# Recurrence of a two-layer hybrid backbone: both heads' keys in the same columns, products as 128x64 tiles, substitution in blocks of 4

## The chip, the cores and the metric

The kernel runs on one core of a Trainium2 chip. The metric is the device time of one execution in microseconds (us). The engines that matter are TensorE (PE; its weight loads are listed as PEld), VectorE (DVE), ScalarE (ACT), GpSimd (POOL) and SyncE (SP), which issues the transfers.

## The reference, cut to what matters

Two layers run over 512 latent tokens and, in the first layer, 256 context tokens as well. Each layer has a mixer (an RWKV-7 recurrence in both directions, windowed attention and a Fourier mix, merged by gates) and a gated ConvFFN. The change concerns the recurrence alone:

```python
def wkv_scan(state0, feat, d, reverse):
    r, v, kk, decays, keys, removals, _ = feat
    def step(S, inp):
        r_t, w_t, k_t, v_t, kk_t, b_t = inp
        sa = jnp.einsum("bhvk,bhk->bhv", S, -kk_t)
        S = S * w_t[:, :, None, :] + sa[..., :, None] * b_t[..., None, :] + v_t[..., :, None] * k_t[..., None, :]
        return S, jnp.einsum("bhvk,bhk->bhv", S, r_t)
```

There are four heads of 64 channels, forward and backward. The kernel works in chunks of 64 tokens: inside a chunk the recurrence is the solution of a unit lower triangular 64x64 system, so that each chunk, head and direction needs the products of its keys with its queries, a triangular inverse, and a few small matmuls that carry the state from chunk to chunk.

## The kernel before, in words

The tokens go through the recurrence in six windows of two chunks in each layer (`mix`, L1329): twelve windows in all. For each window three functions run.

`wkv_features` (L779) runs once per window and loops over the two directions `d`: 24 direction passes. Heads lie in pairs on the partitions: head `h` of a pair has rows 64h to 64h+63, and `k` counts the two pairs. A pass makes decays on ACT and DVE (L822 to L838) and then multiplies them in. `W1[h]` (L851 on DVE, L853 on POOL) holds a head's queries in its own 64 rows; its other rows are zeroed first (L809). `BK` holds both heads' keys; the two kinds of key (`na` and `kf`) lie in crossed column halves for the two heads, so that L854 and L855 are written for each head by itself, as 64-partition instructions. Then L864 makes the products: for each head a bank `ps` takes four matmuls (`q`: two chunks by two pairs) of a 128x128 weight tile of `BK`, with `m` columns moving (128, or 64 where no output is wanted: the first two windows of layer 1, four passes). Out of each bank L869 writes one half of `MR` and L870 one half of the other head's rows of `W1`, both under the triangular mask `gmask` (DVE). POOL then scales `BK` in place (L872).

`wkv_inverse` (L897) runs once per window and inverts all triangles of the window at once. L909 lays out 16x16 diagonal blocks, one per partition. The loop L914 to L919 is a substitution over the 16 rows: for each of 15 columns one multiply (L917) and one add (L919) over what lies below it, 30 dependent DVE instructions. Two transposes (L929, L930) bring the result back, and small 32-row matmuls on PE (L938 to L977) join the 16-blocks to 32 and then to 64.

`wkv_prep` (L980) runs once per chunk, 24 times. It transposes the values (L987) and the scaled keys (L997, four PE transposes of 128x128 into one bank), which ACT copies to `BT`. `wkv_step` (L1002) then carries the state (L1021 to L1063); its matmuls already are 128x64 or 64x64 tiles, put side by side in the array by `tile_position`. While the recurrence runs there are two banks for the tag `x` (the banks `ps`, `pp`, `pv`, `pb` and those of the inverse), one for `y` and five for the projections (L1599).

The order of the work is not written out by hand. Recurrence pieces stand under `tc.high_priority()` (L1369, L1452); the projections and gate matmuls of the same layer (L177 to L179, weights split into a high and a low part by L106 and L118) follow in the program text, and a planner puts them between the recurrence's instructions, by its own estimates, before the run. Each engine then executes its list strictly in that order, and waits on semaphores where an operand is not there yet.

Of the kernel before, what the change touches and what calls it, by code (L numbers as in the profile page):

```python
# [11 lines left out]
ALU = mybir.AluOpType  # L12
AX = mybir.AxisListType
# [50 lines left out]
class Kern:  # L64
# [714 lines left out]
    def wkv_features(self, l, w, F, P, wp, wt):  # L779

        nc = self.nc
        x = P["x"]
        NC = 2
        WT = NC * CH
        W = {}
# [8 lines left out]
        def rows(t, h):  # L794
            return t[64 * h:64 * h + 64]

        for d in range(2):
# [5 lines left out]
            def tok(t):  # L803
                return flip(t[:, :, lo:lo + WT])
# [41 lines left out]
            split = lambda a: a.rearrange("p k (c t) -> p k c t", t=CH)  # L846
            for h in range(2):
                ww = rows(W1[h], h).rearrange("p c k t -> p k c t")
                bk = rows(BK, h).rearrange("p c k t -> p k c t")
                o = 64 * h  # L850
                nc.vector.tensor_tensor(ww[:, :, :, 0:64], split(rows(tok(F["kk"]), h)), rows(e1, h)[:, :, :, 0:64], ALU.mult)  # L851
                if need_y:
                    nc.gpsimd.tensor_tensor(ww[:, :, :, 64:128], split(rows(tok(F["r"]), h)), rows(e1, h)[:, :, :, 1:65], ALU.mult)  # L853
                nc.vector.tensor_tensor(bk[:, :, :, o:o + 64], split(rows(na, h)), split(rows(e2, h)), ALU.mult)  # L854
                nc.vector.tensor_tensor(bk[:, :, :, 64 - o:128 - o], split(rows(kf, h)), split(rows(e2, h)), ALU.mult)  # L855
            vs = self.t(wp, [128, 2, WT + CH], "vs_", bufs=4)
            nc.gpsimd.memset(vs[0:64, :, 0:64], 0.0)
            nc.gpsimd.memset(vs[64:128, :, WT:WT + 64], 0.0)
            self.act(vs[0:64, :, 64:64 + WT], tok(F["v"])[0:64])
            self.act(vs[64:128, :, 0:WT], tok(F["v"])[64:128])  # L860
            for h in range(2):
                ps = self.ps()
                for q in range(4):
                    nc.tensor.matmul(ps[:, q * 128:q * 128 + m], lhsT=BK[:, q // 2, q % 2, :],  # L864
                                     rhs=W1[h][:, q // 2, q % 2, 0:m], start=True, stop=True)
                pv = ps.rearrange("p (q t) -> p q t", q=4)[:, :, 0:m]
                oth = 1 - h
                mask = lambda z: rows(self.gmask, z)[:, 0:m].unsqueeze(1).broadcast_to((64, 4, m))
                nc.vector.tensor_tensor(rows(MR, h)[:, 4 * d:4 * d + 4, 0:m], rows(pv, h), mask(h), ALU.mult)  # L869
                nc.vector.tensor_tensor(rows(W1[h], oth).rearrange("p c k t -> p (c k) t")[:, :, 0:m], rows(pv, oth),  # L870
                                        mask(oth), ALU.mult)
            nc.gpsimd.tensor_tensor(  # L872
                BK, BK, e1[:, :, :, 64].rearrange("p k c -> p c k").unsqueeze(3).broadcast_to((128, NC, 2, 128)), ALU.mult)
            W[d] = (W1, BK, vs, e1)
# [22 lines left out]
    def wkv_inverse(self, MR, wp):  # L897
# [3 lines left out]
        mm = nc.tensor.matmul  # L901
        NI = 8
        Fm = self.t(wp, [128, 16, 32], "iv", bufs=3)
        F16 = self.t(wp, [128, 16, 16], "F16", bufs=1)
        T = self.t(wp, [128, 16, 16], "T16", bufs=1)
        tmp = self.t(wp, [128, 64], "itmp", bufs=1)
        m0, m1, r1 = (self.lmask[:, z:z + 1] for z in (0, 1, 2))

        nc.vector.transpose(Fm.rearrange("l t s -> l (t s)"), MR[:, :, 0:64].rearrange("q i (b t) -> q t b i", b=4))  # L909
        nc.gpsimd.memset(T, 0.0)  # L910
        nc.gpsimd.memset(T.rearrange("l t j -> l (t j)")[:, ::17], 1.0)
        nc.vector.tensor_scalar(F16, Fm[:, :, 0:16], m0, None, ALU.mult)
        nc.vector.scalar_tensor_tensor(F16, Fm[:, :, 16:32], m1, F16, ALU.mult, ALU.add)
        for q in range(15):  # L914
            n, m = 15 - q, q + 1
            t_ = tmp[:, 0:n * m].rearrange("p (a b) -> p a b", b=m)
            nc.vector.tensor_tensor(t_, F16[:, m:16, q:m].broadcast_to((128, n, m)), T[:, q:m, 0:m].broadcast_to((128, n, m)),  # L917
                                    ALU.mult)
            nc.vector.tensor_tensor(T[:, m:16, 0:m], T[:, m:16, 0:m], t_, ALU.add)  # L919
        X1 = self.t(wp, [128, 16, 32], "iv", bufs=3)  # L920
        X2 = self.t(wp, [128, 16, 32], "iv", bufs=3)
        Tt = T.rearrange("l t j -> l j t")
# [57 lines left out]
    def wkv_prep(self, j, W, wp):  # L980

        nc = self.nc
        rows = lambda t, h: t[64 * h:64 * h + 64]
        units = [(d, k) for d in range(2) for k in range(2)]
        pv = self.ps()
        for u, (d, k) in enumerate(units):
            nc.tensor.transpose(pv[:, u * 128:(u + 1) * 128], W[d][2][:, k, j * 64:j * 64 + 128], self.ident)  # L987
        pvv = pv.rearrange("p (u t) -> p u t", u=4)
        ZV = [self.t(wp, [128, 4, 64], f"ZV{h}", bufs=2) for h in range(2)]
        XV = [self.t(wp, [128, 4, 64], f"XV{h}", bufs=2) for h in range(2)]  # L990
        for h in range(2):
            oth = 1 - h
            self.act(rows(ZV[h], oth), rows(pvv, oth)[:, :, 64 * h:64 * h + 64])
            self.act(rows(XV[h], oth), rows(pvv, oth)[:, :, 64 * h:64 * h + 64])
        pb = self.ps()
        for u, (d, k) in enumerate(units):
            nc.tensor.transpose(pb[:, u * 128:(u + 1) * 128], W[d][1][:, j, k, :], self.ident)  # L997
        BT = self.t(wp, [128, 4, 128], "BT", bufs=2)
        self.act(BT, pb.rearrange("p (u t) -> p u t", u=4))
        return ZV, XV, BT  # L1000
# [807 lines left out]
```

## Time and profile before

| what | value |
|---|---|
| runs (3) | 2505.61, 2508.24, 2521.63 us; median 2508.24 |
| the profiled execution's own time | 2513.85 us |
| its span, first to last instruction | 2511.9 us |
| PE busy | 2293.3 us (91% of the span) |
| DVE busy | 1889.0 us (75%) |
| ACT busy, POOL busy | 1052.8 us (42%), 965.1 us (38%) |
| mean granted TensorE clock | 0.965 |

The span is 1.95 us shorter than the execution that it belongs to, which in turn is 5.61 us longer than the median of the runs. Busy times of PE count a matmul to its modelled end, which overlaps the next one's; how fast matmuls follow each other is read from their starts. A plain f32 matmul appears as two records of PE (and two weight loads), an f32 transpose as one. The granted clock has two levels, 2.4 GHz (1.0) and 1.2 GHz (0.5).

The recurrence fills about 160 to 445 us (layer 0) and 1560 to 1820 us (layer 1) of the span.

### The profile page before, as it was taken

The numbers are of one execution on the slowest core, as the hardware profiler recorded it, in microseconds if no ns is written. First come the engines' busy times: TensorE is split into PE (matmuls) and PEld (weight loads), VectorE is DVE, ScalarE is ACT, GpSimd is POOL, SyncE is SP. The second block draws the span as 40 slices with busy tenths as digits, with TensorE's granted clock in tenths as the row PEclk, the third lists the DMA queues.
The fourth block names the chain that finished last, engine by engine and source line by source line (L and its number), as shares of the span: only waits on it lengthen the run. The fifth ranks groups of instructions, "written<-read, shape, count | busy, mean of one in ns | idle before, by whom it ended". The sixth has DMA issues, their size and how long they took to land. (4 is left out here: it accounts for less than half of the span.)

```text
span 2511.9 us, 43604 instructions
## 1 busy us (share of the span) xinstructions
PE 2293.3 (91%) x16612; PEld 1923.1 (77%) x16612; DVE 1889.0 (75%) x3458; ACT 1052.8 (42%) x2153; POOL 965.1 (38%) x965
## 2 busy tenths in 40 slices
PE   7878999999999979999999989889889997899997
PEld 4757777887777768898898777667667776888886
DVE  4967777838866587778778854888667857989988
ACT  3234343335434444343333544435345434544443
POOL 4443322023332363333333544343224424644453
PEclk9989989999999989999999999899999998999999
DMA  7611111644334322222222322112275643322321
GB/s 241 190 51 47 57 37 46 204 146 122 118 122 125 104 67 65 63 72 68 64 69 66 122 93 63 54 59 61 76 211 149 195 128 113 117 88 85 98 89 59
DMA packets 284529, 251.36 MB, mean 100 GB/s; under 512 B 14524, under 2 KB 241300, under 8 KB 284320
## 3 DMA queue, kind: packets, MB, share of 16 engines
q1 hardware_dynamic: 284320, 248.58, 32.0%
q8 instruction: 131, 2.15, 0.4%
q14 instruction: 78, 0.64, 0.1%
HBM read 221.23 MB, written 27.29 MB: 99 GB/s over the span
## 5 line engine op out<-in xcount | busy, mean ns | idle before, releaser
L177 PE MATMUL mm<-at,wh 128*128 128x256 f32 (+2 forms) x1968 | 661.8, 337 | 14.4 <-DVE v L614 7.0
L178 PE MATMUL mm<-at,wh 128*128 128x256 f32 (+2 forms) x1968 | 660.5, 336 | 12.8 <-POOL at L118 7.3
L179 PE MATMUL mm<-at,wl 128*128 128x256 f32 (+2 forms) x1968 | 659.7, 336 | 8.2 <-DVE wl L118 5.9
L118 POOL TENSOR_TENSOR wl<-wr,wh 128x512 fp32r<-128x512 f32 (+1 forms) x248 | 341.8, 1385 | 466.2 <-ACT wh L106 444.0
L177 PEld LDWEIGHTS mm<-at,wh 128*128 128x128 f32 x1968 | 380.8, 194 | 46.9 <-issue 5.6
L178 PEld LDWEIGHTS mm<-at,wh 128*128 128x128 f32 x1968 | 381.1, 194 | 43.4 <-POOL at L118 10.0
L179 PEld LDWEIGHTS mm<-at,wl 128*128 128x128 f32 x1968 | 380.9, 194 | 34.4 <-DVE wl L118 8.9
L106 ACT ACTIVATE wh<-wr 128x512 fp32r<-128x512 f32 (+1 forms) x342 | 204.9, 605 | 235.2 <-PE mm L178 141.3
L118 DVE TENSOR_TENSOR wl<-ws,wh 128x512 fp32r<-128x512 f32 x176 | 166.8, 949 | 65.6 <-ACT wh L106 65.6
L177 PE MATMUL x<-dh,hid 128*128 128x512 f32 x440 | 178.0, 405 | 29.8 <-DVE acc L604 27.7
L295 DVE SCALAR_TENSOR_TENSOR ma<-mw,s,ma 128x256 f32<-128x256 f32 x336 | 187.3, 597 | 11.0 <-DMA mw<-in_mod_w 8.2
L179 PE MATMUL x<-dh,hid 128*128 128x512 f32 x440 | 173.3, 395 | 1.0 <-DVE hid L118 1.0
L178 PE MATMUL x<-dl,hid 128*128 128x512 f32 x440 | 173.2, 394 | 0.0
L604 DVE TENSOR_TENSOR acc<-x,acc 128x512 f32<-128x512 f32 x200 | 134.4, 682 | 24.2 <-PE x L179 23.7
L118 POOL TENSOR_TENSOR dl<-dr,dh 128x1024 fp32r<-128x1024 f32 x44 | 112.2, 2549 | 83.9 <-ACT dh L106 83.9
L106 ACT ACTIVATE wh<-ws 128x512 fp32r<-128x512 f32 x170 | 103.7, 623 | 84.9 <-PE mm L178 70.5
L177 PEld LDWEIGHTS x<-dh,hid 128*128 128x128 f32 x440 | 83.3, 189 | 56.4 <-DVE acc L604 38.6
L154 POOL TENSOR_TENSOR ws<-wr,wr 128x512 f32<-128x512 f32 x42 | 66.4, 1580 | 139.5 <-DVE wl L118 136.9
L178 PE MATMUL x<-at,wh 128*128 128x512 f32 (+2 forms) x312 | 114.4, 367 | 5.0 <-POOL at L118 3.1
L177 PE MATMUL x<-at,wh 128*128 128x512 f32 (+2 forms) x312 | 114.7, 368 | 0.9 <-DVE wh L114 0.7
L106 ACT ACTIVATE P<-P,st 128x513 f32<-128x513 f32 (+5 forms) x120 | 86.0, 722 | 69.8 <-DVE P L1234 58.6
L154 POOL TENSOR_TENSOR ws<-ws,wr 128x512 f32<-128x512 f32 x42 | 62.8, 1495 | 132.5 <-DVE wl L118 75.0
(490 smaller groups left out, 4859.0 us busy)
## 6 DMA issues: line engine op xcount, KB each, us to landing
mw<-in_mod_w SPq DMA_DIRECT2D x96, 512.0 KB, 4.1
wr<-in_ffn_up SPq DMA_DIRECT2D x176, 256.0 KB, 3.1
wr<-in_w_in SPq DMA_DIRECT2D x164, 256.0 KB, 3.0
dr<-in_ffn_down SPq DMA_DIRECT2D x44, 512.0 KB, 3.3
gd<-sg SPq DMA_DIRECT2D x32, 256.0 KB, 2.0
wraw<-in_w_out SPq DMA_DIRECT2D x32, 256.0 KB, 3.7
hd<-h SPq DMA_DIRECT2D x32, 256.0 KB, 2.4
h<-hd SPq DMA_DIRECT2D x28, 256.0 KB, 6.7
```

Of the source, the lines that this page charges most:

```text
L106: return self.nc.scalar.activation(out, in_, func, **kw)
L118: e.tensor_tensor(lo, full, hi.bitcast(F32), ALU.subtract)
L154: e.tensor_tensor(raw[m], raw[x], raw[y], op)
L177: mm(ps, lhsT=lh, rhs=rh, start=first and k == 0, stop=False)
L178: mm(ps, lhsT=lh, rhs=rl, start=False, stop=False)
L179: mm(ps, lhsT=ll, rhs=rh, start=False, stop=last and k == nk - 1)
L295: nc.vector.scalar_tensor_tensor(acc[s], mw[:, k % 4], v, acc[s], ALU.mult, ALU.add)
L604: nc.vector.tensor_tensor(acc[i][:, cs], ps, acc[i][:, cs], ALU.add)
```

## The change: what it does

In `wkv_features` the keys of both heads now lie in the same columns: `na` in columns 0 to 63 of `BK`, `kf` in 64 to 127, so that L854 and L855 become one 128-partition instruction each. The products are made by sixteen matmuls of a 128x64 weight tile in place of eight of 128x128; two banks `pa` and `pb` are held at a time, and the half of `BK` (`z`) and the head decide the bank and the column tile `g` of the array. The bank `pa` then goes to `MR` in one 128-partition instruction under one mask; the halves of `pb` go to `W1` as before.

In `wkv_inverse` the substitution runs over blocks of 4: three columns (six instructions) do all four diagonal 4-blocks at once. The blocks are then joined, 4 to 8 (twice) and 8 to 16 (once): each join is a multiply of n x n x n elements, a sum over the last index, a second multiply and a second sum. That is 18 DVE instructions in place of 30. The scratch tile moves into the tag `iv`, which keeps three buffers.

In `wkv_prep` the four transposes of `BK` become sixteen matmuls with the identity as the moving operand, 64 columns each, which also cross the column halves back for the second head.

```diff
--- before.py
+++ after.py
@@ -846,29 +846,33 @@
             split = lambda a: a.rearrange("p k (c t) -> p k c t", t=CH)
             for h in range(2):
                 ww = rows(W1[h], h).rearrange("p c k t -> p k c t")
-                bk = rows(BK, h).rearrange("p c k t -> p k c t")
-                o = 64 * h
                 nc.vector.tensor_tensor(ww[:, :, :, 0:64], split(rows(tok(F["kk"]), h)), rows(e1, h)[:, :, :, 0:64], ALU.mult)
                 if need_y:
                     nc.gpsimd.tensor_tensor(ww[:, :, :, 64:128], split(rows(tok(F["r"]), h)), rows(e1, h)[:, :, :, 1:65], ALU.mult)
-                nc.vector.tensor_tensor(bk[:, :, :, o:o + 64], split(rows(na, h)), split(rows(e2, h)), ALU.mult)
-                nc.vector.tensor_tensor(bk[:, :, :, 64 - o:128 - o], split(rows(kf, h)), split(rows(e2, h)), ALU.mult)
+            bk = BK.rearrange("p c k t -> p k c t")
+            nc.vector.tensor_tensor(bk[:, :, :, 0:64], split(na), split(e2), ALU.mult)
+            nc.vector.tensor_tensor(bk[:, :, :, 64:128], split(kf), split(e2), ALU.mult)
             vs = self.t(wp, [128, 2, WT + CH], "vs_", bufs=4)
             nc.gpsimd.memset(vs[0:64, :, 0:64], 0.0)
             nc.gpsimd.memset(vs[64:128, :, WT:WT + 64], 0.0)
             self.act(vs[0:64, :, 64:64 + WT], tok(F["v"])[0:64])
             self.act(vs[64:128, :, 0:WT], tok(F["v"])[64:128])
+
+            pa, pb = self.ps(), self.ps()
+            for q in range(4):
+                bq = BK[:, q // 2, q % 2, :]
+                for z, p in ((0, pa), (1, pb)):
+                    for h in range(2):
+                        g = h if z == 0 else 1 - h
+                        nc.tensor.matmul(rows(p, g)[:, q * 128:q * 128 + m], lhsT=bq[:, 64 * z:64 * z + 64],
+                                         rhs=W1[h][:, q // 2, q % 2, 0:m], start=True, stop=True, tile_position=(0, 64 * g))
+            pa, pb = (p.rearrange("p (q t) -> p q t", q=4)[:, :, 0:m] for p in (pa, pb))
+            mask = self.gmask[:, 0:m].unsqueeze(1).broadcast_to((128, 4, m))
+            nc.vector.tensor_tensor(MR[:, 4 * d:4 * d + 4, 0:m], pa, mask, ALU.mult)
             for h in range(2):
-                ps = self.ps()
-                for q in range(4):
-                    nc.tensor.matmul(ps[:, q * 128:q * 128 + m], lhsT=BK[:, q // 2, q % 2, :],
-                                     rhs=W1[h][:, q // 2, q % 2, 0:m], start=True, stop=True)
-                pv = ps.rearrange("p (q t) -> p q t", q=4)[:, :, 0:m]
                 oth = 1 - h
-                mask = lambda z: rows(self.gmask, z)[:, 0:m].unsqueeze(1).broadcast_to((64, 4, m))
-                nc.vector.tensor_tensor(rows(MR, h)[:, 4 * d:4 * d + 4, 0:m], rows(pv, h), mask(h), ALU.mult)
-                nc.vector.tensor_tensor(rows(W1[h], oth).rearrange("p c k t -> p (c k) t")[:, :, 0:m], rows(pv, oth),
-                                        mask(oth), ALU.mult)
+                nc.vector.tensor_tensor(rows(W1[h], oth).rearrange("p c k t -> p (c k) t")[:, :, 0:m], rows(pb, oth),
+                                        rows(mask, oth), ALU.mult)
             nc.gpsimd.tensor_tensor(
                 BK, BK, e1[:, :, :, 64].rearrange("p k c -> p c k").unsqueeze(3).broadcast_to((128, NC, 2, 128)), ALU.mult)
             W[d] = (W1, BK, vs, e1)
@@ -901,22 +905,47 @@
         mm = nc.tensor.matmul
         NI = 8
         Fm = self.t(wp, [128, 16, 32], "iv", bufs=3)
-        F16 = self.t(wp, [128, 16, 16], "F16", bufs=1)
-        T = self.t(wp, [128, 16, 16], "T16", bufs=1)
-        tmp = self.t(wp, [128, 64], "itmp", bufs=1)
+
+        F16f = self.t(wp, [128, 272], "F16", bufs=1)
+        Tf = self.t(wp, [128, 272], "T16", bufs=1)
+        F16, T = (f[:, 0:256].rearrange("l (t s) -> l t s", s=16) for f in (F16f, Tf))
+        tmp = self.t(wp, [128, 16, 32], "iv", bufs=3).rearrange("l t s -> l (t s)")
+        pr = self.t(wp, [128, 64], "ipr", bufs=1)
         m0, m1, r1 = (self.lmask[:, z:z + 1] for z in (0, 1, 2))
 
         nc.vector.transpose(Fm.rearrange("l t s -> l (t s)"), MR[:, :, 0:64].rearrange("q i (b t) -> q t b i", b=4))
         nc.gpsimd.memset(T, 0.0)
-        nc.gpsimd.memset(T.rearrange("l t j -> l (t j)")[:, ::17], 1.0)
+        nc.gpsimd.memset(Tf[:, 0:256:17], 1.0)
         nc.vector.tensor_scalar(F16, Fm[:, :, 0:16], m0, None, ALU.mult)
         nc.vector.scalar_tensor_tensor(F16, Fm[:, :, 16:32], m1, F16, ALU.mult, ALU.add)
-        for q in range(15):
-            n, m = 15 - q, q + 1
-            t_ = tmp[:, 0:n * m].rearrange("p (a b) -> p a b", b=m)
-            nc.vector.tensor_tensor(t_, F16[:, m:16, q:m].broadcast_to((128, n, m)), T[:, q:m, 0:m].broadcast_to((128, n, m)),
-                                    ALU.mult)
-            nc.vector.tensor_tensor(T[:, m:16, 0:m], T[:, m:16, 0:m], t_, ALU.add)
+
+        def blocks(f, n):
+
+            x = 17 * n
+            v = f[:, 0:16 // n * x].rearrange("l (b x) -> l b x", x=x)[:, :, 0:16 * n]
+            return v.rearrange("l b (t s) -> l b t s", s=16)
+
+
+        F4, T4 = blocks(F16f, 4), blocks(Tf, 4)
+        for q in range(3):
+            n, m = 3 - q, q + 1
+            t_ = tmp[:, 0:4 * n * m].rearrange("p (c a b) -> p c a b", c=4, b=m)
+            nc.vector.tensor_tensor(t_, F4[:, :, m:4, q:m].broadcast_to((128, 4, n, m)),
+                                    T4[:, :, q:m, 0:m].broadcast_to((128, 4, n, m)), ALU.mult)
+            nc.vector.tensor_tensor(T4[:, :, m:4, 0:m], T4[:, :, m:4, 0:m], t_, ALU.add)
+
+        for n in (4, 8):
+            F8, T8 = blocks(F16f, 2 * n), blocks(Tf, 2 * n)
+            for c in range(8 // n):
+                lo, up = F8[:, c, n:2 * n, 0:n], T8[:, c, 0:n, 0:n]
+                t_ = tmp[:, 0:n ** 3].rearrange("p (t j s) -> p t j s", j=n, s=n)
+                p_ = pr[:, 0:n * n].rearrange("p (t j) -> p t j", j=n)
+                nc.vector.tensor_tensor(t_, lo.unsqueeze(2).broadcast_to((128, n, n, n)),
+                                        up.rearrange("p s j -> p j s").unsqueeze(1).broadcast_to((128, n, n, n)), ALU.mult)
+                nc.vector.tensor_reduce(p_, t_, AX.X, ALU.add)
+                nc.vector.tensor_tensor(t_, T8[:, c, n:2 * n, n:2 * n].unsqueeze(2).broadcast_to((128, n, n, n)),
+                                        p_.rearrange("p s j -> p j s").unsqueeze(1).broadcast_to((128, n, n, n)), ALU.mult)
+                nc.vector.tensor_reduce(T8[:, c, n:2 * n, 0:n], t_, AX.X, ALU.add)
         X1 = self.t(wp, [128, 16, 32], "iv", bufs=3)
         X2 = self.t(wp, [128, 16, 32], "iv", bufs=3)
         Tt = T.rearrange("l t j -> l j t")
@@ -994,7 +1023,11 @@
             self.act(rows(XV[h], oth), rows(pvv, oth)[:, :, 64 * h:64 * h + 64])
         pb = self.ps()
         for u, (d, k) in enumerate(units):
-            nc.tensor.transpose(pb[:, u * 128:(u + 1) * 128], W[d][1][:, j, k, :], self.ident)
+            for h in range(2):
+                for z, g in ((0, h), (1, 1 - h)):
+                    nc.tensor.matmul(rows(pb, g)[:, u * 128 + 64 * h:u * 128 + 64 * h + 64],
+                                     lhsT=W[d][1][:, j, k, 64 * z:64 * z + 64], rhs=self.ident[:, 64 * h:64 * h + 64],
+                                     start=True, stop=True, tile_position=(0, 64 * g))
         BT = self.t(wp, [128, 4, 128], "BT", bufs=2)
         self.act(BT, pb.rearrange("p (u t) -> p u t", u=4))
         return ZV, XV, BT
```

## Rows read from the trace of the kernel before

**Rows 1.** The page, part 1: busy us (share of the span) and instructions of PE.
```profile
PE 2293.3 (91%) x16612; PEld 1923.1 (77%) x16612; DVE 1889.0 (75%) x3458; ACT 1052.8 (42%) x2153; POOL 965.1 (38%) x965
```

**Rows 2.** Windows: stretch, its length, busy us (records) by engine, granted clock.
```profile
core 0: us, PE busy (x) PEld busy (x) DVE busy (x) ACT busy (x) POOL busy (x), PEclk, DMA share, GB/s
160.00:445.00 285.00, 255.66 (x3317) 208.51 (x3316) 213.37 (x511) 107.34 (x276) 91.82 (x155) 0.92 0.17 52
1560.00:1820.00 260.00, 234.61 (x2980) 180.08 (x2979) 211.04 (x511) 110.88 (x277) 89.64 (x147) 0.94 0.20 63
1660.00:1780.00 120.00, 111.42 (x1525) 85.39 (x1525) 108.48 (x266) 58.88 (x150) 44.94 (x86) 1.00 0.22 69
354.00:374.00 20.00, 18.75 (x302) 14.48 (x302) 11.62 (x37) 6.96 (x18) 1.84 (x5) 0.66 0.13 36
```

**Rows 3.** Waits of PE, whole span: us in total, times, longest us.
```profile
PE x L864 <- DVE BK L855: 28.8, 15, 4.1
...
PE x L864 <- DVE BK L854: 9.9, 2, 6.3
PE x L864 <- POOL W L853: 8.7, 6, 2.1
```

**Rows 4.** PE groups by line, whole span: busy us, mean ns, idle before.
```profile
L864 PE MATMUL x<-W,BK 128*128 128x128 f32 (+1 forms) x384 | 62.1, 328 | 47.4 <-DVE BK L855 28.8 <-DVE BK L854 9.9 <-POOL W L853 8.7
...
L997 PE MATMUL x<-ident,BK 128*128 128x128 f32 x96 | 16.0, 289 | 0.6 <-DVE TTt L977 0.6
```

**Rows 5.** Timeline of PE, several places: start us, us, weight tile, moving columns, records.
```profile
222.59 0.66 PE L997 MATMUL x<-ident,BK 128*128 128x128 f32 x4 [0.62 <-DVE TTt L977]
223.17 0.33 PE L1021 MATMUL y<-ZV,W 128*64 128x64 f32 x2
...
231.36 0.61 PE L814 MATMUL x<-xa,a 128*128 128x128 f32 x4
231.90 0.69 PE L1047 MATMUL y<-W,ZV 128*64 128x64 f32 x16
232.52 0.68 PE L1052 MATMUL y<-MR,XV 64*64 64x64 f32 x16
...
254.88 2.02 PE L864 MATMUL x<-W,BK 128*128 128x128 f32 x16 [0.71 <-DVE BK L855]
256.66 0.36 PE L178 MATMUL mm<-at,wh 128*128 128x256 f32 x1
...
358.20 0.49 PE L948 MATMUL x<-TTt,Ps 32*16 32x16 f32 x41 [1.25 <-issue]
...
584.17 1.09 PE L1268 MATMUL a<-PT,vt 128*64 128x128 f32 x14
585.19 0.39 PE L1222 MATMUL s<-ka,qa 128*128 128x256 f32 x1
...
1586.68 1.97 PE L864 MATMUL x<-W,BK 128*128 128x64 f32 x16 [0.50 <-DVE BK L855]
```

**Rows 6.** DVE groups, whole span: busy us, mean ns, idle before.
```profile
L919 DVE TENSOR_TENSOR T<-T,itmp 128x15 f32<-128x15 f32 (+4 forms) x180 | 42.2, 235 | 5.5
L917 DVE TENSOR_TENSOR itmp<-F,T 128x15 f32<-128x15 f32 (+4 forms) x180 | 41.9, 233 | 5.5
...
L869 DVE TENSOR_TENSOR MR<-x,table 64x512 f32<-64x512 f32 (+1 forms) x48 | 30.8, 642 | 24.8 <-PE x L864 24.8
L854 DVE TENSOR_TENSOR BK<-wt,wt 64x256 f32<-64x256 f32 x48 | 30.5, 635 | 0.5 <-ACT wt L106 0.3
L855 DVE TENSOR_TENSOR BK<-wt,wt 64x256 f32<-64x256 f32 x48 | 29.3, 609 | 2.1 <-ACT wt L106 2.0
L836 DVE TENSOR_TENSOR wt<-wt,k 128x256 f32<-128x256 f32 x24 | 10.6, 442 | 2.7 <-ACT wt L106 2.4
```

**Rows 7.** DVE groups with shapes apart, whole span: a sum-like pass and a 128x512 product.
```profile
L1234 DVE TENSOR_SCALAR_CACHE_REDUCE P<-s 128x513 f32<-128x513 f32 x32 | 22.0, 687 | 13.6 <-PE s L1228 13.1 <-POOL wl L118 0.3
...
L1148 DVE TENSOR_TENSOR mm<-mm,sin 128x512 f32<-128x512 f32 x10 | 6.9, 697 | 3.5 <-PE mm L1147 3.4
```

## The prediction

> **What bounds the kernel now.** I began with the page: TensorE is busy for 91% of the span and VectorE for 75% [rows 1], so over the whole kernel a microsecond of TensorE work is the first thing to count. A share of busy time is a mean over stages, so next came the windows of the two stretches in which the recurrence runs [rows 2]. There TensorE is busy 255.7 of 285 us and 234.6 of 260 us, VectorE 213.4 and 211.0 us. In the steady part of layer 1 (1660 to 1780 us, three windows of the recurrence of 40 us each) both are nearly full: 111.4 and 108.5 of 120 us. The recurrence alone would not fill TensorE; the projections placed between its instructions do. What TensorE loses there stands in two views. Its waits name one line above all, L864, the products of this change: 28.8 + 9.9 us behind the key multiplications on VectorE, in 15 + 2 waits, and 8.7 us behind POOL, in 6 [rows 3], together the 47.4 us of idle time of that group [rows 4]. And the granted clock is 0.92 and 0.94 of full speed in the two stretches [rows 2], that is about 285 x 0.08 + 260 x 0.06 = 38 us of clock lost. The work that the recurrence doesn't do runs later on the same TensorE, so I count: the time changes by the work added to TensorE, less the stalls that go.
>
> **Products, 24 passes.** Today a pass has 8 matmuls, 16 records; from 254.88 to the next line's start at 256.66 they take 1.78 us, 0.111 each [rows 5]. The change makes 16 matmuls of half a weight tile, 32 records. The nearest row is L1268, 128x64 tiles side by side with 128 columns moving: 14 records from 584.17 to 585.19, 1.02 us [rows 5]. In that is a change of tile shape. Its price: four records of L814 take 0.54 us up to L1047 (231.36 to 231.90) where 4 x 0.111 = 0.44 would do, so 0.10 us [rows 5]. A record of L1268 thus costs (1.02 - 0.10) / 14 = 0.066 us, and a pass 32 x 0.066 + 2 x 0.10 = 2.31 us, 0.53 more. For the 20 passes with 128 columns that is +10.6 us. In the four passes with 64 columns the same records cost no less today (1.97 against 2.02 us for 16 [rows 5]), about 1.73 to the next start; after, by L1047's 16 records of 64 columns in 0.62 us with one change in it (0.0325 each [rows 5]), 32 x 0.0325 + 0.20 = 1.24. That is -0.5 x 4 = -2.0 us.
>
> The Trainium skill, TensorEngine Tiling (Array Packing), section Overview, gives up to twofold speed for a dimension of 64 or less, so that two half tiles would cost one full one. The row says 0.066 against 0.111 / 2 = 0.0555, a factor of 1.7. By the page the 20 passes would add only their changes of shape, 4 us and not 10.6; the measurement decides.
>
> **Keys turned, 24 preps.** Four transposes (one record each, 96 in all [rows 4]) take 0.58 us up to the next tiled group, 0.10 of it a change of shape [rows 5]. The new form has 16 matmuls of two records, 32 x 0.0325 = 1.04 us, and one or two changes: 1.14 against 0.58 beside a tiled group, 1.24 against 0.48 between full tiles. I take the middle, +0.66 x 24 = +15.8 us. TensorE in all: 10.6 - 2.0 + 15.8 = +24.4 us at full speed, and at the clock of these stretches (0.93) **+26 us**. Bounds: were all changes of shape hidden and the pairs perfect, about +10; were two tiles not side by side at all, over +80, which the rows of L1268 and L1047 exclude. I keep +10 to +30.
>
> **Keys multiplied.** L854 and L855 take 635 and 609 ns, 48 times each [rows 6]. A pass loses one of each, 1.24 us; a 128-partition instruction of the same 256 columns costs no more (L836, 442 ns [rows 6]). These are what L864 waits for in 17 waits: at most 17 x 1.24 = 21 us of TensorE's idle time go. At least nothing goes, since the planner places L864 by its estimates and will place it earlier by what it believes is saved; then the wait, which is the error of its estimate, stays. The six waits on POOL's L853 stay in any case. I take two thirds, **-14 us**: the missing instructions are also ones that are drawn out today (635 against 442 ns). Next late behind them is L853.
>
> **Mask and bank.** L869 takes 30.8 us in 48 [rows 6]; 20 x 0.70 (by L1148 [rows 7]) + 4 x 0.44 remain, so VectorE gains 15 us. I value this at nothing, because the first bank is now ready only after all 32 records, 2.3 us, where today it is ready after 8, 0.9 us. The last of L870 then ends at 2.31 + 3 x 0.69 = 4.4 us after the start, today 0.9 + 4 x 0.68 = 3.6. The two banks of tag `x` are both held that long, and L814, L938 and the preps queue behind them on TensorE. Projections in the five other banks cover it; without that cover it costs 0.8 x 24 = 19 us. That end goes to the slow side.
>
> **Substitution, 12 windows.** Today 30 instructions take (42.2 + 41.9 + 5.5 + 5.5) / 12 = 7.9 us [rows 6]. After: 6 + 8 short ones at 0.23 + 0.03, 3.7 us, and four passes over 512 elements at 0.69 + 0.03 (L1148 for the products; for the sums the nearest is L1234, 687 ns over 513 elements [rows 7]), 2.9 us: 6.6, saving 1.3 x 12 = 16 us of VectorE. If a sum over an index took twice that row's time, 1.4 us more, nothing would be saved. VectorE is not the only thing TensorE follows here, and filler covers most of it: I take a quarter, **-4 us**. The extra tenant of `iv` waits for nothing: when the result of the inverse is laid out, the scratch is done with.
>
> **Sum.** 26 - 14 - 4 = +8 us on the profiled execution's 2513.85, 2522; that execution stands 5.6 us over the median, so the forecast for the median is 2508.24 + 8 = **2516 us**. Without any relief it is +26, with all of the 21 and 16 it is -11: the case's own range is 2497 to 2534.
>
> **Rivals.**
> *VectorE is the pacemaker (faster).* For it: 108.5 of 120 us busy in the steady part [rows 2]. A window loses 2 x 1.24 + 2 x 0.63 + 1.3 = 5.0 us of VectorE, 60 us over twelve. If TensorE follows it, the waits of L864 go altogether (47 us [rows 4]) and with them half of the 38 us of clock, 19: 26 - 47 - 19 = -40, 2468 us. Against it: in the same part TensorE is busy for 111.4 us, and the planner, not VectorE, sets how early L864 stands. Chance 0.22.
>
> *TensorE's list stalls (slower).* The change adds 24 x (16 + 28) = 1056 records, with as many weight loads. At 358.20 the list stood still for 1.25 us with nothing to wait for [rows 5], and over the 20 us around it the granted clock is 0.66, at 1.2 GHz for most of it [rows 2]: 20 x 0.34 = 6.8 us, with the stall 8 us for one event. Should no relief come (+26) and two more such events, the sum is 26 + 16 = +42, 2550 us. It decides from the point where the relief is under 1 us: from there the kernel is slower by over 1% without any event. For it: L864's long waits are planned ones; against: five such groups of tiled matmuls per chunk already run without one. Chance 0.20.
>
> *The transposes (a little better).* In the stretch from 354 to 374 us at a granted clock of 0.66 [rows 2], two of the 24 groups of L997 run. If matmuls in their place end such a stretch, its 6.8 us come back: 2516 - 7 = 2509. The Trainium skill, TensorE: Matmul & The Clock Gate, section Part 4 (PE-mode transpose), says that the transpose mode does not count as work for the clock as matmuls do; no row here separates that from the stall at 358.20. Chance 0.05.
>
> **How the numbers follow.** Forecast 0.53, rivals 0.22, 0.20 and 0.05. A measurement of this kernel can tell about 1%, 25 us, from no change. Faster by over that: the first rival and 0.01 of the forecast, 0.23. Slower: the second rival and 0.03 of the forecast, 0.23. Within: 0.54. The range reaches to the middle of either rival, 2470 to 2550; the likeliest case's own is 2497 to 2534.
>
> **What would show it.** Right: the products with 32 records in about 2.3 us a pass and the turned keys in 1.1 to 1.2 a prep; L854 and L855 with 24 each at about 0.5 us; 18 short and long instructions of substitution in 6 to 7 us; L864's idle time down from 47 to about 33 us; TensorE's busy time up. Wrong: that idle time near zero and a higher clock (the first rival), or new waits with no releaser and a clock under 0.92 (the second). If the tiled records take 0.11 us each, the sum fails at its first term.

## The result and the profile after

The changed kernel takes 2534.24 us (median of 5 runs, 2528.66 to 2538.61) against 2508.24, a ratio of 1.0096 with a 95% interval of 1.0073 to 1.0119: slower by 26 us. I had said 2516, within 2470 to 2550. The profiled execution took 2533.03 us with a span of 2531.2, 19.3 us over the span of before. The page of after, part 1, in the columns of [rows 1]:

```profile
PE 2313.2 (91%) x17668; PEld 1933.9 (76%) x17668; DVE 1852.5 (73%) x3242; ACT 1050.7 (42%) x2153; POOL 957.8 (38%) x965
```

1056 more records on TensorE, as counted, and 20 us more of busy time; VectorE has 37 us less. The windows of after, in the columns of [rows 2] (the last line is the end of layer 0's recurrence):

```profile
160.00:445.00 285.00, 250.99 (x3664) 202.26 (x3664) 189.77 (x393) 103.64 (x270) 91.35 (x154) 0.92 0.14 44
1560.00:1820.00 260.00, 227.53 (x3440) 176.57 (x3440) 198.67 (x410) 120.19 (x293) 92.42 (x165) 0.96 0.17 52
1660.00:1780.00 120.00, 108.24 (x1720) 82.70 (x1721) 95.99 (x201) 54.64 (x142) 43.71 (x85) 0.97 0.16 50
425.00:470.00 45.00, 44.26 (x504) 31.25 (x500) 10.19 (x26) 8.51 (x20) 1.62 (x5) 0.92 0.20 61
```

In the steady part VectorE fell from 108.5 to 96.0 of 120 us, and the kernel still became slower: VectorE did not set the pace there (e7 below tests it). The waits of TensorE after, as [rows 3], and then its two groups, as [rows 4]:

```profile
PE x L867 <- DVE BK L853: 38.0, 17, 6.3
...
PE x L867 <- POOL W L851: 12.7, 11, 2.1
```
```profile
L867 PE MATMUL x<-W,BK 128*64 128x128 f32 (+1 forms) x768 | 57.9, 304 | 51.0 <-DVE BK L853 38.0 <-POOL W L851 12.7
L1028 PE MATMUL x<-ident,BK 128*64 128x64 f32 x768 | 31.6, 229 | 0.9 <-ACT BT L106 0.6
```

L867 is the products (L864 before), L1028 the turned keys (L997 before). The products wait 51.0 us where they waited 47.4, still in 17 places for a key multiplication, now L853. The turned keys have doubled. One pass and one prep on TensorE's timeline of after, then one alternation in it that [rows 5] don't have:

```profile
1660.12 2.08 PE L867 MATMUL x<-W,BK 128*64 128x128 f32 x32 [2.23 <-DVE BK L853]
1662.13 0.50 PE L177 MATMUL mm<-at,wh 128*128 128x512 f32 x1
...
1754.36 1.15 PE L1028 MATMUL x<-ident,BK 128*64 128x64 f32 x32
1755.44 0.68 PE L1061 MATMUL y<-q,TTt 64*64 64x64 f32 x14
```
```profile
434.88 0.28 PE L179 MATMUL mm<-at,wl 128*128 128x256 f32 x1
435.00 0.28 PE L177 MATMUL mm<-at,wh 128*128 128x256 f32 x1
...
435.44 0.33 PE L1028 MATMUL x<-ident,BK 128*64 128x64 f32 x2
435.70 0.39 PE L177 MATMUL mm<-at,wh 128*128 128x256 f32 x1
436.02 0.33 PE L1028 MATMUL x<-ident,BK 128*64 128x64 f32 x2
436.27 0.39 PE L178 MATMUL mm<-at,wh 128*128 128x256 f32 x1
```

A pass takes 2.01 us, a prep 1.08. From 435.70 to 436.27, 0.57 us, stand one projection (0.12 by 434.88 to 435.00) and two records of 0.0325; the other 0.39 us are two changes of tile shape, twice the 0.10 each that the prediction took from L814. In the kernel before such groups run there as blocks:

```profile
436.47 0.69 PE L1047 MATMUL y<-W,ZV 128*64 128x64 f32 x16
437.08 0.68 PE L1052 MATMUL y<-MR,XV 64*64 64x64 f32 x16
...
438.82 0.69 PE L1021 MATMUL y<-ZV,W 128*64 128x64 f32 x16
```

Where does the alternation come from? The planner takes the instruction with the lower number first. The recurrence's second block in layer 0 has the numbers 0 to 1793 before and 0 to 1881 after; the projections beside it start at 958. So the last windows stand among the projections' numbers, and a longer recurrence reaches further in. Layer 1's projections start near 10000, and nothing crosses.

The substitution after (groups with shapes apart; 12 windows):

```profile
L946 DVE TENSOR_TENSOR iv<-T,ipr 128x512 f32<-128x512 f32 x12 | 13.2, 1103 | 0.2
L943 DVE TENSOR_TENSOR iv<-F,T 128x512 f32<-128x512 f32 x12 | 12.5, 1045 | 0.4
L948 DVE TENSOR_REDUCE T<-iv 128x64 f32<-128x512 f32 x12 | 8.2, 686 | 0.4
L945 DVE TENSOR_REDUCE ipr<-iv 128x64 f32<-128x512 f32 x12 | 8.2, 683 | 0.3
```

The table splits TensorE's time in each profiled execution, from each record's start to the next one's, less idle time; what no column names adds up to some 300 us. "Other tiled" is the rest of the recurrence from the inverse on; "projections" are L177 to L179. Median and ratio are of all runs of a kernel, and so is "clock lost": a run's span times what its mean granted clock lacks to full speed, averaged over the runs (for the kernel before, its runs beside the experiments). That is the most that the lower level of the clock can have cost, since idle time at it costs nothing.

| kernel | median us | ratio, 95% | products | keys turned | other tiled | projections | idle before products | other idle | clock lost |
|---|---|---|---|---|---|---|---|---|---|
| before | 2508.2 | | 57.2 | 12.4 | 130.1 | 1790.1 | 47.4 | 153.8 | 89 |
| after | 2534.2 | 1.0073-1.0119 | 54.2 | 28.4 | 134.3 | 1795.5 | 51.0 | 149.7 | 88 |
| e1 | 2510.2 | 1.0007-1.0044 | 57.3 | 12.5 | 127.3 | 1785.0 | 50.9 | 149.3 | 90 |
| e2 | 2574.3 | 1.0240-1.0293 | 54.8 | 32.9 | 146.6 | 1828.1 | 50.6 | 151.1 | 117 |
| e3 | 2507.0 | 0.9977-1.0009 | 57.9 | 11.8 | 126.6 | 1791.1 | 50.7 | 150.9 | 81 |
| e4 | 2504.7 | 0.9971-1.0007 | 49.8 | 26.7 | 129.6 | 1795.6 | 37.4 | 141.1 | 78 |
| e5 | 2535.9 | 1.0082-1.0121 | 55.7 | 27.2 | 126.8 | 1789.4 | 50.7 | 165.2 | 93 |
| e6 | 2533.6 | 1.0068-1.0136 | 57.8 | 11.8 | 138.6 | 1805.1 | 48.6 | 147.4 | 98 |
| e7 | 2535.3 | 1.0074-1.0125 | 56.8 | 28.2 | 132.8 | 1797.8 | 55.7 | 146.1 | 81 |
| e8 | 2486.4 | 0.9891-0.9930 | 48.5 | 11.8 | 127.5 | 1790.4 | 35.5 | 151.9 | 79 |
| e9 | 2502.6 | 0.9953-0.9998 | 52.0 | 11.8 | 128.8 | 1790.7 | 33.1 | 158.5 | 93 |
| e10 | 2489.0 | 0.9901-0.9949 | 50.5 | 12.5 | 127.6 | 1784.2 | 35.0 | 153.5 | 80 |
| e11 | 2473.6 | 0.9852-0.9891 | 48.2 | 11.8 | 124.9 | 1788.7 | 34.8 | 147.5 | 68 |
| e12 | 2507.4 | 0.9980-1.0015 | 49.6 | 26.6 | 124.1 | 1792.2 | 37.2 | 154.5 | 79 |

Before to after: keys +16.0, other tiled +4.2, projections +5.4, products -3.0, everything else -2.6, idle time -0.5. That is +19.5, the span's 19.3. The kernel before ran at 2508 to 2510 us beside every experiment.

### The profile page after: what moved, and what is told of

Same layout as the page of the kernel before. It is cut to its first block, busy times and chain, and to the rows that moved or that the text cites. A ratio compares the mean times of both kernels' runs of the same rounds, so it can differ in the third digit from the quotient of the medians.

```text
span 2531.2 us, 45519 instructions
## 1 busy us (share of the span) xinstructions
PE 2313.2 (91%) x17668; PEld 1933.9 (76%) x17668; DVE 1852.5 (73%) x3242; ACT 1050.7 (42%) x2153; POOL 957.8 (38%) x965
## 5 line engine op out<-in xcount | busy, mean ns | idle before, releaser
L177 PE MATMUL mm<-at,wh 128*128 128x256 f32 (+2 forms) x1968 | 663.1, 337 | 17.1 <-DVE v L614 6.7
L179 PE MATMUL mm<-at,wl 128*128 128x256 f32 (+2 forms) x1968 | 661.4, 336 | 10.9 <-DVE wl L118 7.2
L177 PEld LDWEIGHTS mm<-at,wh 128*128 128x128 f32 x1968 | 380.1, 193 | 51.1 <-issue 10.5
L179 PEld LDWEIGHTS mm<-at,wl 128*128 128x128 f32 x1968 | 380.0, 193 | 39.5 <-DVE wl L118 10.9
L177 PE MATMUL x<-dh,hid 128*128 128x512 f32 x440 | 177.7, 404 | 30.2 <-DVE acc L604 28.4
L295 DVE SCALAR_TENSOR_TENSOR ma<-mw,s,ma 128x256 f32<-128x256 f32 x336 | 185.8, 592 | 15.0 <-DMA mw<-in_mod_w 12.4
L179 PE MATMUL x<-dh,hid 128*128 128x512 f32 x440 | 172.9, 394 | 1.0 <-DVE hid L118 1.0
L604 DVE TENSOR_TENSOR acc<-x,acc 128x512 f32<-128x512 f32 x200 | 134.3, 682 | 23.5 <-PE x L179 22.9
L177 PEld LDWEIGHTS x<-dh,hid 128*128 128x128 f32 x440 | 83.1, 189 | 56.7 <-DVE acc L604 39.3
L177 PE MATMUL x<-at,wh 128*128 128x512 f32 (+2 forms) x312 | 115.6, 371 | 0.7 <-DVE wh L114 0.7
L179 PE MATMUL x<-at,wl 128*128 128x512 f32 (+2 forms) x312 | 114.4, 367 | 0.0
```

Of the source, the lines that this page charges most:

```text
L177: mm(ps, lhsT=lh, rhs=rh, start=first and k == 0, stop=False)
L179: mm(ps, lhsT=ll, rhs=rh, start=False, stop=last and k == nk - 1)
L295: nc.vector.scalar_tensor_tensor(acc[s], mw[:, k % 4], v, acc[s], ALU.mult, ALU.add)
L604: nc.vector.tensor_tensor(acc[i][:, cs], ps, acc[i][:, cs], ALU.add)
```

## The experiments

**Which part costs: e1, e2, e3.** e1 is the kernel before with only the diff's part in `wkv_inverse`; e2 is the changed kernel with the old one:

```diff
-        for q in range(15):
...
+        F4, T4 = blocks(F16f, 4), blocks(Tf, 4)
...
```

> The kernel before with the blocked substitution alone. Theory (the loss is TensorE work added in the turned keys, and the relief on VectorE buys next to nothing): 2505 us, between 2498 and 2512. Rival (the joins with sums over an index are themselves slower on the path that counts): 2514 to 2522.

> The changed kernel with the old substitution over 16 rows. Theory: the substitution is worth little, 2537 us, between 2530 and 2544, TensorE idle before the products still about 50 us. Rival (the new substitution is what costs): 2520 to 2528.

e1: 2510.16 us, inside the theory's range, near its upper end; the substitution alone is worth nothing here. e2: 2574.29 us, a miss of both. Its recurrence has 12 instructions more in each window, so its numbers reach further among the projections'; TensorE's alternation is longer there, and the clock fell on it. The window of e2, then two turns of the alternation in it:

```profile
429.60:467.00 37.40, 37.40 (x194) 22.80 (x193) 3.99 (x10) 4.10 (x10) 0.98 (x3) 0.50 0.08 26
```
```profile
440.45 0.23 PE L952 MATMUL x<-TTt,Ps 32*16 32x16 f32 x2
440.61 0.58 PE L177 MATMUL mm<-at,wh 128*128 128x256 f32 x1
441.12 0.23 PE L952 MATMUL x<-TTt,Ps 32*16 32x16 f32 x2
```

TensorE counts as busy for all of 37.40 us and is granted 0.50, the lower level of 1.2 GHz. So e2 says little of the substitution.

e3 is the changed kernel with four transposes a prep again; the second head's halves are crossed while GpSimd scales them (three instructions for one, and a copy on ScalarE):

```diff
-            for h in range(2):
-                for z, g in ((0, h), (1, 1 - h)):
...
+            nc.tensor.transpose(pb[:, u * 128:(u + 1) * 128], W[d][1][:, j, k, :], self.ident)
...
+            nc.gpsimd.tensor_tensor(rows(bx, 1), rows(BK, 1)[:, :, :, 0:64], ..., ALU.mult)
+            nc.gpsimd.tensor_tensor(rows(BK, 1)[:, :, :, 0:64], rows(BK, 1)[:, :, :, 64:128], ..., ALU.mult)
...
+            self.act(rows(BK, 1)[:, :, :, 64:128], rows(bx, 1))
```

> The changed kernel with four transposes of 128x128 in the preparation as before; the halves of the second head's keys are crossed while they are scaled (three instructions on POOL, one on ACT in place of one on POOL). Theory: the 16 us that TensorE spends more on the turned keys go, 2518 us, between 2513 and 2524. Rival (TensorE had room for them in layer 1, where the changed kernel lost nothing): 2526, half of it. Rival (the longer chain on POOL and ACT is late for the state): above 2530.

2506.97 us, 27 less than after and lower than expected. The keys fall from 28.4 to 11.8, other tiled by 7.7, projections by 4.4; the alternation is gone as well. From e1 to e3 products, keys' layout, mask and the crossing differ: -3 us, no more than the scatter of the runs, with 9 us less of clock lost. So with the substitution and the new products the kernel stands where it stood, and the turned keys, with the alternation that they bring along, carry the whole loss.

**The alternation: e6, e5, e12.** The numbers of layer 0's recurrence alone are moved: in e6 in the kernel before, upwards (176 for 0), in e5 in the changed one, below all others.

```diff
-        with tc.high_priority():
+        with tc.high_priority(offset=tc.cur_priority - 176 if l == 0 else None):
```

```diff
-        with tc.high_priority():
+        with tc.high_priority(offset=tc.cur_priority + 5000 if l == 0 else None):
```

> The kernel before with one difference: in layer 0 the second block of the recurrence takes numbers that begin at 176 instead of 0 in the planner, about as if 176 instructions had been added ahead of it. No instruction is added or taken away; TensorE's list gets 93 more changes of tile shape (843 for 750), all of them near the end of layer 0's recurrence. Theory (the numbering alone makes the alternation, and the alternation costs): 93 x 0.39/2 = 18 us more than the kernel before, 2526 us (2518 to 2540; the upper end if the clock falls to half in the stretch), although no work was added. Rival (only the added work costs): 2506 to 2511 us.

> The changed kernel with one difference: in layer 0 the two blocks of the recurrence take numbers 5000 lower in the planner, so that all of them stand below the numbers of the other matmuls (which begin at 958), instead of running from 0 to 1881 across them. No instruction is added or taken away; TensorE's list has 74 fewer changes of tile shape (757 for 831), all of them near the end of layer 0's recurrence. Theory (what was lost beyond the turned keys is the alternation of tiled records with single untiled matmuls there, which the trace puts at 0.39 us for two changes): 74 x 0.39/2 = 14 us less than the changed kernel, 2520 us (2514 to 2526), with no stretch of alternating pairs at 430 to 470 us. Rival (the alternation lies beside waits that are there anyway, and the loss is the products' and turned keys' own length): 2530 to 2536 us.

e6: 2533.58 us, +25 with not one instruction added. Its window, below the same one of before:

```profile
425.00:470.00 45.00, 44.33 (x453) 34.19 (x442) 30.43 (x71) 20.00 (x33) 0.10 (x1) 1.00 0.52 166
425.00:470.00 45.00, 45.00 (x294) 29.98 (x294) 6.43 (x15) 7.26 (x16) 0.10 (x1) 0.85 0.18 53
```

294 records for 453 in the same 45 us: the alternation and a clock of 0.85. That the numbering makes it and that it costs is shown for the kernel before. But e5, in the changed kernel, missed: 2535.92 us. TensorE's groups gave back 14.8 us (keys 1.2, other tiled 7.5, projections 6.1), the 14 expected; other idle time rose by 15.5, and the runs of e5 lost 5 us more to the clock than after's. Nearly half of the idle time is one wait, in e5's waits of TensorE and on its timeline:

```profile
PE x L311 <- DVE ma L295: 6.9, 1, 6.9
```
```profile
468.65 1.95 PE L311 MATMUL x<-ones,ma 128*128 128x1 f32 x16 [0.54 <-DVE y L1140]
477.45 1.83 PE L311 MATMUL x<-ones,ma 128*128 128x1 f32 x8 [6.86 <-DVE ma L295]
```

The recurrence ends earlier, and the sums of a modulation row, next on TensorE's list, wait for VectorE. e12 is e5's edit on e4 (below).

> The changed kernel with the queries on VectorE (2505 us by itself) and with the recurrence of layer 0 numbered below the other work. TensorE's list has 54 fewer changes of tile shape than without the numbering (782 for 836). Theory (each change costs TensorE 0.2 us, 11 us in all, but what is gained turns into a wait for VectorE's modulation sums right behind the recurrence, as it did without the queries' move): 2500 to 2507 us, with a wait of over 4 us on those sums. Rival (the wait was an accident of that one order): 2490 to 2497 us.

2507.42 us, the time at the edge of the theory's range (e4: 2504.74), the place not: other tiled -5.5, projections -3.4, other idle +13.4, but the waits of L311 come to 0.7 us in all. The idle time is spread over many later waits. In both runs the freed time turned into idle time; why it spreads stays open. So in the changed kernel the alternation, taken away alone, gives no time back.

**The waits before the products: e7, e4, e9, e10.** e7 writes the two key multiplications of after twice.

```diff
             nc.vector.tensor_tensor(bk[:, :, :, 0:64], split(na), split(e2), ALU.mult)
             nc.vector.tensor_tensor(bk[:, :, :, 64:128], split(kf), split(e2), ALU.mult)
+            nc.vector.tensor_tensor(bk[:, :, :, 0:64], split(na), split(e2), ALU.mult)
+            nc.vector.tensor_tensor(bk[:, :, :, 64:128], split(kf), split(e2), ALU.mult)
```

> The changed kernel with the two multiplications that make the shared key columns (0.63 us each on VectorE) written twice, the second time over the first with the same values: 24 x 1.27 = 30 us of VectorE work more, at the end of the chain that the products wait for. Theory (the chain of VectorE sets when the products start, as their waits of 38.0 us in 17 places on that line say): idle before the products grows from 51 to 66 to 80 us, and the time to 2548 to 2562 us. Rival (the order on TensorE's list sets it, and the preparation is done early enough in most windows): idle within 5 us of 51, and 2534 to 2539 us.

2535.29 us; idle time before the products 51.0 to 55.7, with 19 us more of VectorE's busy time. The rival holds: the plan places the products later by what it believes was added, and the wait, its error, stays. The order in the traces bears this out: ahead of the last pass TensorE has run 6106 records of the projections (L177 to L179) in the kernel before, 6053 in after, 6069 in e7. The change moved the products up in the list, and e7 moved them down again. With 7 us less of clock lost than after, e7's extra work may have cost about that much; the theory wanted 14 to 28. e4 (after), e9 (before) and e10 (e1) have the queries on VectorE:

```diff
-                    nc.gpsimd.tensor_tensor(ww[:, :, :, 64:128], ...
+                    nc.vector.tensor_tensor(ww[:, :, :, 64:128], ...
```

> The changed kernel with the multiplication of the queries by the decays moved from POOL to VectorE (40 instructions of 64x256). Theory (TensorE's wait before the products is an error of the plan, made by VectorE and POOL slowing each other): the idle time before the products falls from 51 us to under 30, the key multiplications take 0.45 us and not up to 0.9, and the time is 2515 to 2525. Rival (the wait follows the length of VectorE's chain): 40 x 0.42 = 17 us more on VectorE, idle time 51 us or more, 2540 to 2550.

> The kernel before with one difference: the queries times their decays on VectorE instead of GpSimd. Theory (the late queries are no matter of the change; they draw out the preparation on either side of it, as the waits of 8.7 us on that line before and 12.7 after say): idle time before the products falls from 47 to 33 to 38 us as it did in the changed kernel (51 to 37), and the time by 10 to 20 us, to 2494 us (2488 to 2500). Rival (the gain of 30 us in the changed kernel was the end of its alternation of tiled records with others, which the kernel before hardly has): 2504 to 2512 us.

> The kernel before with the blocked substitution and with the queries on VectorE. Theory (the substitution is worth nothing by itself, as with the queries on GpSimd, where it measured +2 us): the time of the kernel before with the queries on VectorE, within 5 us. Rival (with 0.75 us a head and window more on VectorE the 9 us that the blocked substitution saves there count): 6 to 12 us less than that kernel.

The idle time before the products falls by 14 to 16 us in each pair (51.0 to 37.4, 47.4 to 33.1, 50.9 to 35.0). The time falls by 30, 6 and 21. e4 went below its 2515 to 2525 us, though the idle time stayed above the 30 expected. e9's idle time came as expected and its time did not: in the traces other idle time grew by 4.7 us and TensorE's lines outside the table by 5, and the runs lost 4 us more to the clock. e10 is 13.6 us below e9, just past the rival's 6 to 12. But that is not VectorE's shorter work shown: its runs lost 12 to 13 us less to the clock than e9's (80 against 93), which is nearly the whole difference, and the one run of e9 with e10's mean clock, 0.968, took 2487.58 us. Why the clock fell less often in e10 stays open. The queries among the groups of GpSimd before, then, with the key multiplications, among VectorE's in e9:

```profile
L853 POOL TENSOR_TENSOR W<-r,e 64x256 f32<-64x256 f32 x40 | 33.3, 833 | 32.1 <-ACT e L106 30.2
```
```profile
L854 DVE TENSOR_TENSOR BK<-wt,wt 64x256 f32<-64x256 f32 x48 | 25.2, 525 | 0.5 <-ACT wt L106 0.3
L855 DVE TENSOR_TENSOR BK<-wt,wt 64x256 f32<-64x256 f32 x48 | 24.3, 507 | 1.7 <-ACT wt L106 1.7
L853 DVE TENSOR_TENSOR W<-r,e 64x256 f32<-64x256 f32 x40 | 21.6, 540 | 0.0
```

The multiplication is shorter there, and its neighbours on VectorE are too (635 and 609 ns before [rows 6]). Taken one by one, 43 of the 96 key multiplications of before run beside no GpSimd instruction other than a memset and take 418 ns, at most 425; the other 53 overlap one and take 788. In e9, 66 of 96 run alone.

**Put together: e8, e11.** e8 is e3 and e4 together. In e11 the crossing moves to the copy out of PSUM:

```diff
-        self.act(BT, pb.rearrange("p (u t) -> p u t", u=4))
+        pv = pb.rearrange("p (u t) -> p u t", u=4)
+        self.act(BT[:, :, 0:64], pv[:, :, 0:64])
+        self.act(rows(BT, 0)[:, :, 64:128], rows(pv, 1)[:, :, 64:128])
+        self.act(rows(BT, 1)[:, :, 64:128], rows(pv, 0)[:, :, 64:128])
```

> The changed kernel with both single alterations together: four transposes a window and head pair for the keys, the second head's halves crossed while they are scaled (was 27 us less than the changed kernel by itself), and the queries times their decays on VectorE instead of GpSimd (was 30 us less by itself). Theory (the two act at different places: the one takes the doubled matmuls of the turned keys, the other the late queries before the products; but both had also taken the alternation at 430 to 470 us, which can go only once, about 14 us): 2534 - 27 - 30 + 14 = 2491 us (2483 to 2500), faster than the kernel before. Rival (each of them had its gain from the one alternation alone): 2503 to 2510 us.

> The changed kernel with the queries on VectorE and with four transposes for the keys, the second head's halves crossed by ScalarE as it copies them out of PSUM (three instructions instead of one), so that the scaling on GpSimd stays one instruction. TensorE's work is that of the version with the crossing on GpSimd (2486 us). Theory (copies of half the rows on ScalarE, busy for 42% of the span, are hidden, and 48 fewer instructions on GpSimd help): 2480 to 2487 us. Rival (the copies stand between the transposes and the step that waits for them; 24 x 2 x 0.3 us more there): 2492 to 2500 us.

e8: 2486.36 us, as the sum said. e11: 2473.63 us, ratio 0.9871, better than expected and 35 us below before, the best of all; of its 13 us below e8 up to 11 are the clock's (68 lost against 79). From e4 to e8 the turned keys go: -18 us. From e10 to e8 come the new products: -3, within the scatter, as from e1 to e3.

## Why the prediction was right or wrong

The direction and the range held; the forecast was 18 us short. The time came out at what the prediction gives for no relief at all, +26, and that is luck: the products came 11.6 us under their term and the neighbours 8.0 over theirs. By its steps:

- *Keys turned, +15.8*: 16.0 measured, 1.2 of it the alternation (e5); 1.08 us a prep for 1.14. Right.
- *Products, +10.6 - 2.0*: -3.0. A full-speed pass takes 2.01, not 2.31. The record of L1268 [rows 5] was too dear a price: (2.01 - 0.20) / 32 = 0.057 us, near 0.111 / 2. I had misread that row: its 14 records start in pairs, 0.109 us from pair to pair (0.055 a record), but the last two, at 584.88 and 584.99, run without a partner. The Trainium skill, TensorEngine Tiling (Array Packing), section Overview, gives up to twofold speed, which I had set aside; here the trace agrees with it. By passes, the four with 64 columns fell from 10.4 to 6.2 us, the other twenty rose from 46.8 to 48.0: where a full-speed pass costs 0.2 more, fewer of them ran at the lower clock (over 3 us: six before, four after).
- *Neighbours, nothing but 1.6 for the clock*: other tiled +4.2, projections +5.4. This was not in the sum. On TensorE's lines it is the alternation at the end of layer 0's recurrence, where the numbers cross: e5 takes 13.6 us off the two. I had read the list as fixed. But e5's time did not fall, so what part of the 26 us the alternation made is not shown.
- *Relief of the waits, -14*: the failed step. The idle time rose by 3.6 with 1.24 us a pass taken away, and e7, with them added, moved it by 4.7. I had written the reason down as the lower bound (the plan places the products by its estimates) and still took two thirds.
- *Substitution, -4 from a quarter of 16*: VectorE saved 95 - 86 = 9 us. The products over 512 elements, whose operands repeat and are read across, take 1.05 and 1.10 us where the row for L1148 gave 0.70 [rows 7]; the sums, 0.69, were right. Worth +2 alone (e1); the -14 with the queries on VectorE (e10) go with the clock, not with VectorE's work.
- *Mask and bank, nothing*: L871's 15.5 us in place of L869's 30.8 [rows 6] bought nothing visible; no run tried it alone.

The rivals: VectorE as pacemaker falls by the steady part, 108.5 to 96.0 us without a gain, and by e7. The stalled list had the right sign but not the mechanism: idle time of TensorE that nothing in the profile ends is 3.9 us before and 7.2 after, and the granted clock of the two stretches is no lower (0.92 and 0.96). The transposes' clock: the time lost by granted clocks below full, over the whole span, is 84.3 us in the profiled execution of after and 84.9 in that of e3 with the transposes back, so nothing came from there.

## What to carry to other kernels

An engine's wait at the end of another engine's chain is not proof that a shorter chain helps; where a planner places the waiter by estimates, write the suspected instruction twice and see whether the wait moves. Before a few microseconds are put down to a change, compare the granted clock of the runs: here it made nearly the whole difference between e9 and e10. Price a change of layout by every place that reads it: here shared columns made the products no dearer and four transposes into 32 records, and crossing the halves in a copy on a half-idle engine gave it back. When instructions are added to a block with numbers of its own, look where its numbers meet those of the work beside it. And when a row prices tiles that run side by side, look whether each record in it has a partner.

## What the runs showed of the chip

- Two changes of tile shape around a single matmul cost 0.39 us. The Trainium skill, TensorEngine Tiling (Array Packing), section Tiling Modes, says that changing the mode drains TensorE; it gives no price, and the trace agrees with the rule.
- In e2 TensorE counts as busy without a gap for 37.4 us, for the most part alternating pairs of 32x16 or 32x32 records with single projections, and stayed at the lower level of its clock all along.
- With the queries' multiplication moved from GpSimd (833 ns) to VectorE (540), VectorE's own key multiplications became about 100 ns shorter each. The Trainium skill, SBUF — State Buffer, section SBUF: two separate sides, says that a VectorE instruction with two SBUF inputs and one of GpSimd that reads SBUF lock each other out. The trace agrees: 418 ns alone, 788 beside a GpSimd instruction.
- On VectorE the two products of the last join, with one operand repeated and the other read across its rows and repeated, take 1.05 and 1.10 us over 512 elements; L1148 takes 0.70 [rows 7]. No run separates the repeating from the reading across.
